# Where a feed-forward layer's first step takes its fourth weight operand from, and the order of the last tile's work before it

## The chip, the cores and the metric

The kernel runs on one core of one Trainium2 chip. Its metric is the time of one execution on the device in microseconds (us), lower is better. TensorE (PE in the profile) multiplies matrices, VectorE (DVE), ScalarE (ACT) and GpSimd (POOL) work on whole tiles of 128 partitions, and SP only issues transfers.

## The reference

One encoder layer over 1280 tokens (256 of a prompt, 1024 of a sample), width 1024. The change lies at the seam between the two steps below: the end of the attention part's output projection and the start of the FFN.

```python
    mix = jnp.concatenate([rmsnorm(a, mla_out_g), rmsnorm(b, na_out_g)], axis=-1)
    x = x + mix @ w_o
    h2 = rmsnorm(x, ffn_norm_g)
    x = x + (jax.nn.silu(h2 @ w_gate) * (h2 @ w_up)) @ w_down
```

All of it is float32: w_o is 1024 x 1024, w_gate and w_up are 1024 x 2816, w_down is 2816 x 1024.

## The kernel before

**Three matmuls for one.** Each float32 operand is split into a high half, a cast to the matmul type, and a low half, the raw value less the high half. `mm3` (L108) multiplies high by high (L110), high by low (L111) and low by high (L112). `split_S` (L890) does this for the token side, high by ScalarE (L892), low by VectorE (L893). `split_A` (L896) does it for weights, high by ScalarE (L899), low by GpSimd (L900), into six buffers named "wc".

**Seven products for eight.** Gate and up projections are done block by block with a seven-product scheme of fast matrix multiplication. Tokens fall into two halves of 640, the model width into two halves, and the columns go in pairs of 128: one step `fp` does a pair for gate (i = 0) and for up (i = 1), and there are eleven steps. For product m, TensorE multiplies a token operand S*m* by a weight operand. Operands of products 1 and 2 are blocks as they are ("11" and "12"), so they are free of sums; those of 6, 3, 5 and 7 are sums of blocks, which GpSimd builds (`sum_A`, L909, at L910). `product` (L966) does one half (s) of 320 tokens in 12 matmuls, so one operand has 24. The order is `SEQ = (1, 2, 6, 7, 4, 5, 3)`. Product 2 adds onto product 1's sum in PSUM (`CHAIN`), once ScalarE has copied that sum out (L980).

**The tiles before.** The loop at L936 walks over ten token tiles: `mix_T` and `out_proj` for the projection, then `ffn_in` (L840): x is squared (L844) and stored, `rstd_of` (L87) makes the reciprocal root on GpSimd (L89, L91), VectorE scales x (L847), TensorE transposes it (L856), VectorE and ScalarE scale the two transposed halves with the gains gf into the blocks R["11"] to R["22"] (L859, L863), named zA and zB in the trace. From tile 5 on, `difference` (L877) makes the block differences that the token operands need. T2[0] to T2[4], under the names A21, A22, sum, sum and A12, are the five cuts of S6, of 128 tokens each. Tile 8's are made by GpSimd, the last tile's by VectorE.

**The first FFN step.** Step 0 is written out by hand. Its first four operands are (gate, 1), (gate, 2), (up, 1) and (up, 2). Three are split while the tiles run (L941 to L945), which takes all six wc buffers; the block of the fourth, up's "12", is loaded at tile 7 into the buffer A12. The fourth is split inside the step:

```python
                if (i, m) == (1, 1):
                    w0[2, 1] = operand(A0[1], 2)
                    A0[1]["12"] = load_A(1, 0, "12", at[5])
                    w6 = [operand(A0[0], 6, at[6], "A21")]
                    hold = w6[0][2]
```

`hold` is the cast of gate's operand 6; the copies (L980) of the third and fourth operand's products come after it on ScalarE. The other blocks of step 0 and some of the sums lie in `at`, eight pieces of the two buffers that later hold S5. `build_S` (L1013) makes S6 (called at L1053), S7, S4, S5 and S3.

**Who sets the order.** SP's queue follows the program. On the other engines a planner lists the instructions before the run, by readiness as it reckons it and by program order; each engine then works through its list in order. `tc.issue_after(x)` puts what follows behind x in the planner's order. Pools are laid out end to end: the FFN pools (`l4a`: S6, 20 KB per partition; `l4z`: z, 20 KB; `l4b`: S5, S7, S4, 20 KB each) lie over the released pools of the tiles (gm and eight output weights of 8 KB, mT0 of 8 KB, then gf, three 4 KB buffers m and small ones, mT1, two x), and a buffer waits for those that it covers.

Of the kernel before, what the change touches and what calls it, by code (L numbers as in the profile page):

```python
# [11 lines left out]
F32 = mybir.dt.float32  # L12
F32R = mybir.dt.float32r
AF = mybir.ActivationFunctionType
# [25 lines left out]
def encoder_trunk(ctx: ExitStack, tc: tile.TileContext, x_tm, x_T, g_attn, w_c, w_v, w_qk,  # L40
# [46 lines left out]
    def rstd_of(out, ss, n):  # L87
        w = out.shape[1]
        nc.gpsimd.tensor_scalar(out=out, in0=ss, scalar1=1.0 / n, scalar2=EPS,  # L89
                                op0=ALU.mult, op1=ALU.add)  # L90
        nc.gpsimd.tensor_tensor(out=out, in0=out, in1=mhalf[:, 0:w], op=ALU.pow)  # L91

# [697 lines left out]

    mixed = [None]

# [47 lines left out]
    def ffn_in(t, x):  # L840
        h2 = rm.tile([P, D], F32, name="m", bufs=3)
        ss = rm.tile([P, 1], F32, name="ssh", bufs=2)
        r = rm.tile([P, 1], F32, name="rh", bufs=2)
        nc.scalar.activation(h2, x, AF.Square, accum_out=ss)  # L844
        store(xm_d[t], x)
        rstd_of(r, ss, D)
        nc.vector.tensor_scalar(out=h2, in0=x, scalar1=r, scalar2=1.0, op0=ALU.mult,  # L847
# [24 lines left out]
        difference(eng, R["11"][:, :, cs], R["12"][:, :, cs], R["11"][:, :, cs])  # L872
        difference(eng, T2[t - 5], R["22"][:, :, cs], R["11"][:, :, cs])
        if t < NT - 2:
# [21 lines left out]
    def split_A(raw):  # L896
        hi = rY.tile([P, 4, P], F32R, name="wc", bufs=6)
        lo = rY.tile([P, 4, P], F32R, name="wc", bufs=6)
        i0 = nc.scalar.copy(out=hi, in_=raw)  # L899
        i1 = nc.gpsimd.tensor_tensor(out=lo, in0=raw, in1=hi, op=ALU.subtract)  # L900
        return hi, lo, i0.ins, i1.ins
# [62 lines left out]

    l4 = [pool("l4a"), pool("l4z"), pool("l4b")]
    def product(C, w, m, s, held, bank=None, hold=None):  # L966
# [46 lines left out]
    def build_S(m, after):  # L1013
        pl, nm = {6: (l4[0], "S6"), 3: (rA, "zA")}.get(m, (l4[2], f"S{m}"))
        S[m] = [pl.tile([P, 4, NQ], F32R, name=nm, bufs=2) for x in "hl"]
        cuts = [(slice(n * P, (n + 1) * P), T2[n]) for n in range(5)] if m == 6 else [
            (slice(s * NS, (s + 1) * NS), None) for s in range(2)]
        for cs, from_ in cuts[:-1] if m == 6 else cuts:
            after = split_after(m, cs, from_, after)
        return after  # L1020
# [31 lines left out]

    s6 = build_S(6, ())  # L1053
    with tc.issue_after(s6[1]):
        cs8 = slice(3 * P, 4 * P)
        difference(nc.vector, R["21"][:, :, cs8], R["21"][:, :, cs8], T2[3])
    for fp in range(NF // 2):
# [3 lines left out]
        if fp == 0:  # L1061
            spare = [l4[2].tile([P, 4, NQ], F32R, name="S5", bufs=2).bitcast(F32)
                     .rearrange("p a b -> p (a b)").rearrange("p (n a b) -> p n a b", n=5, b=P)
                     for _ in range(2)]
            at = [spare[n // 5][:, n % 5] for n in range(8)]
            for n, (b, i) in enumerate((("21", 0), ("22", 0), ("21", 1), ("22", 1), ("12", 0),
# [3 lines left out]
            for i, m in ((0, 1), (0, 2), (1, 1), (1, 2)):  # L1070
                if (i, m) == (1, 1):
                    w0[2, 1] = operand(A0[1], 2)
                    A0[1]["12"] = load_A(1, 0, "12", at[5])
                    w6 = [operand(A0[0], 6, at[6], "A21")]
                    hold = w6[0][2]
                    s6 = split_after(6, slice(4 * P, 5 * P), T2[4], (hold, s6[1]))
                    with tc.issue_after(s6[1]):
                        difference(nc.vector, R["12"][:, :, cs8], R["22"][:, :, cs8],
                                   R["12"][:, :, cs8])
                        differences(nc.vector, NT - 1)  # L1080
# [307 lines left out]
```

## Time and profile before

| | us |
|---|---|
| median of 3 runs | 1619.09 |
| lowest and highest | 1615.41, 1620.34 |
| the profiled execution | 1617.07 |
| its span, first to last instruction | 1615.2 |

| engine | busy us | share of the span |
|---|---|---|
| PE matmul | 1582.2 | 98% |
| PE weight load | 1444.1 | 89% |
| DVE | 891.1 | 55% |
| ACT | 715.5 | 44% |
| POOL | 664.7 | 41% |

Shares are means over stages with different limits. The tile loop ends and the first FFN step begins at about 797 us of the span; the names M, z and zB (in L980, L982) mark the FFN's sums, S all token operands. The profile doesn't tell buffers of one name apart.

### The profile page before, as it was taken

The page shows a single profiled execution, that of the slowest core. Times are in us where ns is not written, and L with a number is a line of the kernel's source. Part 1 is how long each engine was busy: PE and PEld are TensorE (multiplying, and loading weights), DVE is VectorE, ACT ScalarE, POOL GpSimd, SP SyncE. Part 2 cuts the span into 40 slices and gives each one's busy share as a digit, 9 for nine tenths or more (in the row PEclk, how much of TensorE's full clock was granted, in tenths as well). Part 3 has the DMA queues.
Part 4 walks back from the last instruction along what each step waited for, and adds up shares of the span by engine and source line. Part 5 has one row for each costly group of instructions (what it writes and reads, how often), then busy time and mean ns, then how long its engine had stood idle before and what let it go on. Part 6 is the DMA issues. An engine that isn't in the chain of part 4 may idle for free.

```text
span 1615.2 us, 25739 instructions
## 1 busy us (share of the span) xinstructions
PE 1582.2 (98%) x9616; PEld 1444.1 (89%) x9616; DVE 891.1 (55%) x1483; ACT 715.5 (44%) x1484; POOL 664.7 (41%) x815
## 2 busy tenths in 40 slices
PE   8989999999999999999999999999999999999998
PEld 8978899998888888888899999999999998888886
DVE  5853054456677787533484444334444246886676
ACT  6533154455677777644353223232222332443334
POOL 4631434544211119224676665665656651010002
PEclk9999999999999999999999999999999999999999
DMA  8635202143101030233312232232332237843534
GB/s 293 200 90 141 49 24 63 35 168 102 32 16 30 21 113 16 92 118 143 118 58 72 97 110 93 62 100 84 101 110 70 76 128 264 298 140 97 157 103 155
DMA packets 123246, 171.12 MB, mean 106 GB/s; under 512 B 35504, under 2 KB 67504, under 8 KB 123120
## 3 DMA queue, kind: packets, MB, share of 16 engines
q1 hardware_dynamic: 78880, 120.30, 24.1%
q10 hardware_dynamic: 43680, 46.87, 8.4%
q0 software_dynamic: 560, 2.29, 0.3%
q8 instruction: 76, 1.25, 0.3%
q14 instruction: 50, 0.41, 0.1%
HBM read 118.96 MB, written 50.46 MB: 105 GB/s over the span
## 4 chain that ended last, share of the span: by engine, by line
PE 88%; DVE 3%; issue 2%; ACT 2%; POOL 2%; DMA 1%; ACTq 0%; SPq 0%; POOLq 0%; DVEq 0%
PE M L110 11%; PE M L112 11%; PE M L111 11%; PE d L111 5%; PE d L110 5%; PE d L112 5%; PE o L718 4%; PE tp L708 3%; PE na_o L489 2%; PE po L110 2%; PE po L111 2%; PE po L112 2%; PE pj L110 2%; PE pj L111 2%; PE pj L112 2%
## 5 line engine op out<-in xcount | busy, mean ns | idle before, releaser
L110 PE MATMUL M<-S,wc 128*128 128x320 f32 x1056 | 322.1, 310 | 2.5 <-ACT S L892 1.2
L111 PE MATMUL M<-S,wc 128*128 128x320 f32 x1056 | 324.3, 309 | 0.0
L112 PE MATMUL M<-S,wc 128*128 128x320 f32 x1056 | 312.1, 309 | 0.0
L110 PEld LDWEIGHTS M<-S,wc 128*128 128x128 f32 x1056 | 197.9, 188 | 3.7 <-ACT wc L899 1.6
L111 PEld LDWEIGHTS M<-S,wc 128*128 128x128 f32 x1056 | 198.8, 188 | 0.0
L112 PEld LDWEIGHTS M<-S,wc 128*128 128x128 f32 x1056 | 195.3, 188 | 0.0
L900 POOL TENSOR_TENSOR wc<-A,wc 128x512 fp32r<-128x512 f32 x86 | 120.6, 1403 | 81.5 <-ACT wc L899 81.4
L982 DVE TENSOR_TENSOR z<-M,z 128x320 f32<-128x320 f32 x120 | 56.6, 487 | 128.3 <-PE M L112 112.8
L899 ACT CAST wc<-A 128x512 fp32r<-128x512 f32 x86 | 53.5, 622 | 162.2 <-PE M L111 146.3
L900 POOL TENSOR_TENSOR wc<-sum,wc 128x512 fp32r<-128x512 f32 x62 | 88.6, 1430 | 85.7 <-ACT wc L899 85.7
L111 PE MATMUL d<-S,S 128*128 128x512 f32 (+1 forms) x314 | 121.2, 386 | 0.0
L112 PE MATMUL d<-S,S 128*128 128x512 f32 (+1 forms) x314 | 120.7, 386 | 0.0
L110 PE MATMUL d<-S,S 128*128 128x512 f32 (+1 forms) x314 | 120.4, 387 | 0.0
L982 DVE TENSOR_TENSOR zB<-M,zB 128x320 f32<-128x320 f32 x100 | 47.5, 488 | 131.7 <-PE M L112 125.3
L100 DVE TENSOR_TENSOR PT<-tp,PT 128x512 fp32r<-128x512 f32 (+1 forms) x144 | 93.0, 657 | 39.0 <-ACT PT L99 37.8
L899 ACT CAST wc<-sum 128x512 fp32r<-128x512 f32 x62 | 38.4, 619 | 143.2 <-PE M L111 94.5
L99 ACT CAST PT<-tp 128x512 fp32r<-128x512 f32 (+1 forms) x144 | 79.3, 565 | 38.3 <-PE tp L708 34.6
L700 DVE TENSOR_REDUCE mm<-S 128x1 f32<-128x1024 f32 (+1 forms) x80 | 84.8, 1061 | 10.9 <-PE S L112 9.3
L1029 ACT CAST S<-as 128x640 fp32r<-128x640 f32 x58 | 42.2, 728 | 105.6 <-issue 60.2
L702 ACT ACTIVATE ex<-S,mm 128x1024 f32<-128x1024 f32 (+1 forms) x80 | 79.7, 996 | 8.0 <-DVE mm L700 7.4
L731 POOL TENSOR_TENSOR ob<-ob 128x128 f32<-128x128 f32 x40 | 18.5, 462 | 157.3 <-ACT ob L728 153.8
L718 PE MATMUL o<-PT,v 128*128 128x256 f32 x544 | 80.6, 287 | 1.0 <-ACT PT L99 1.0
(429 smaller groups left out, 4118.1 us busy)
## 6 DMA issues: line engine op xcount, KB each, us to landing
as<-act_d SPq DMA_DIRECT2D x73, 320.0 KB
w<-in_w_down_dram SPq DMA_DIRECT2D x44, 256.0 KB
act_d<-z ACTq DMA_DIRECT2D x35, 320.0 KB
act_d<-zB ACTq DMA_DIRECT2D x35, 320.0 KB
A<-in_w_gate_dram SPq DMA_DIRECT2D x42, 256.0 KB
A<-in_w_up_dram SPq DMA_DIRECT2D x42, 256.0 KB
x<-in_x_tm_dram SPq DMA_DIRECT2D x20, 512.0 KB
cT_d<-stg ACTq DMA_DIRECT2D x20, 320.0 KB
```

Of the source, the lines that this page charges most:

```text
L99: i = nc.scalar.copy(out=hi, in_=ps)
L100: nc.vector.tensor_sub(out=lo, in0=ps, in1=hi)
L110: nc.tensor.matmul(out, lhsT=sh, rhs=mh, start=first, stop=False, **kw)
L111: nc.tensor.matmul(out, lhsT=sh, rhs=ml, start=False, stop=False, **kw)
L112: return nc.tensor.matmul(out, lhsT=sl, rhs=mh, start=False, stop=last, **kw).ins
L700: nc.vector.reduce_max(out=nm[:, u:u + 1], in_=S, axis=AX.X, negate=True)
L702: nc.scalar.activation(ex, S, AF.Exp, bias=nm[:, u:u + 1], scale=1.0, accum_out=l[:, u:u + 1])
L708: nc.tensor.transpose(tp[:, j], ex[:, kt * P:(kt + 1) * P], ident)
L718: nc.tensor.matmul(oT, lhsT=vv, rhs=pt[s][g][:, j], start=kt == 0 and s == 0, stop=kt == nkt - 1 and s == 1)
L899: i0 = nc.scalar.copy(out=hi, in_=raw)
L900: i1 = nc.gpsimd.tensor_tensor(out=lo, in0=raw, in1=hi, op=ALU.subtract)
L982: nc.vector.tensor_add(out=o, in0=ps, in1=a)
```

## The change

There are four edits. The second difference of tile 8, T2[3], is no longer made inside `ffn_in` but after the loop, on GpSimd still, behind the last tile's reciprocal root (`last_rs`). The first cast of S6 is put behind the last tile's square (`last_sq`). The fourth operand's halves get a place of their own, two pieces of the second S5 buffer, and are split before the step begins, the low half by VectorE. The pool of S5, S7 and S4 becomes three pools (`l4b`: two S5; `l4c`: S7's high half; `l4d`: two S4 and S7's low half), and the three pieces of `at` that lay in the second S5 buffer now lie in the first S4 buffer and in S7's high one.

```diff
--- before.py
+++ after.py
@@ -88,7 +88,7 @@
         w = out.shape[1]
         nc.gpsimd.tensor_scalar(out=out, in0=ss, scalar1=1.0 / n, scalar2=EPS,
                                 op0=ALU.mult, op1=ALU.add)
-        nc.gpsimd.tensor_tensor(out=out, in0=out, in1=mhalf[:, 0:w], op=ALU.pow)
+        return nc.gpsimd.tensor_tensor(out=out, in0=out, in1=mhalf[:, 0:w], op=ALU.pow).ins
 
     def split_w(hi, lo, raw):
         nc.gpsimd.tensor_scalar(out=hi, in0=raw, scalar1=1.0, scalar2=1.0, op0=ALU.mult,
@@ -788,7 +788,7 @@
             split_w(wt[:, 0], wt[:, 1], raw)
             wo.append(wt)
 
-    mixed = [None]
+    mixed, last_sq, last_rs = [None], [None], [None]
 
     def mix_in(t):
         ts_ = slice(t * P, (t + 1) * P)
@@ -841,9 +841,9 @@
         h2 = rm.tile([P, D], F32, name="m", bufs=3)
         ss = rm.tile([P, 1], F32, name="ssh", bufs=2)
         r = rm.tile([P, 1], F32, name="rh", bufs=2)
-        nc.scalar.activation(h2, x, AF.Square, accum_out=ss)
+        last_sq[0] = nc.scalar.activation(h2, x, AF.Square, accum_out=ss).ins
         store(xm_d[t], x)
-        rstd_of(r, ss, D)
+        last_rs[0] = rstd_of(r, ss, D)
         nc.vector.tensor_scalar(out=h2, in0=x, scalar1=r, scalar2=1.0, op0=ALU.mult,
                                 op1=ALU.mult)
         c0 = (t % 5) * P
@@ -870,7 +870,8 @@
         T2[t - 5] = rY.tile([P, 4, P], F32, name=nm, bufs=2 if nm == "sum" else 1)
         eng = nc.vector if t == NT - 1 else nc.gpsimd
         difference(eng, R["11"][:, :, cs], R["12"][:, :, cs], R["11"][:, :, cs])
-        difference(eng, T2[t - 5], R["22"][:, :, cs], R["11"][:, :, cs])
+        if t != NT - 2:
+            difference(eng, T2[t - 5], R["22"][:, :, cs], R["11"][:, :, cs])
         if t < NT - 2:
             differences(eng, t)
 
@@ -894,8 +895,7 @@
         return i0.ins, i1.ins
 
     def split_A(raw):
-        hi = rY.tile([P, 4, P], F32R, name="wc", bufs=6)
-        lo = rY.tile([P, 4, P], F32R, name="wc", bufs=6)
+        hi, lo = [rY.tile([P, 4, P], F32R, name="wc", bufs=6) for _ in range(2)]
         i0 = nc.scalar.copy(out=hi, in_=raw)
         i1 = nc.gpsimd.tensor_tensor(out=lo, in0=raw, in1=hi, op=ALU.subtract)
         return hi, lo, i0.ins, i1.ins
@@ -962,7 +962,7 @@
              4: ((1, 0), (0, 1)), 5: ((1, 1), (1, 1)), 3: ((0, 1), (0, 1))}
     DONE = {2: (0, 0), 4: (1, 0), 5: (1, 1), 3: (0, 1)}
 
-    l4 = [pool("l4a"), pool("l4z"), pool("l4b")]
+    l4 = [pool("l4a"), pool("l4z"), pool("l4b"), pool("l4c"), pool("l4d")]
     def product(C, w, m, s, held, bank=None, hold=None):
         bank = 1 - s if bank is None else bank
         if m not in CHAIN:
@@ -1011,8 +1011,9 @@
             (store_p if fp == NF // 2 - 1 else store)(act_d[n][fp], out)
 
     def build_S(m, after):
-        pl, nm = {6: (l4[0], "S6"), 3: (rA, "zA")}.get(m, (l4[2], f"S{m}"))
-        S[m] = [pl.tile([P, 4, NQ], F32R, name=nm, bufs=2) for x in "hl"]
+        pl, nm = {6: (l4[0], "S6"), 3: (rA, "zA"), 5: (l4[2], "S5")}.get(m, (l4[4], "S4"))
+        S[m] = [pl.tile([P, 4, NQ], F32R, name=nm, bufs=2) if m != 7 else
+                l4[3 + n].tile([P, 4, NQ], F32R, name="S7") for n in range(2)]
         cuts = [(slice(n * P, (n + 1) * P), T2[n]) for n in range(5)] if m == 6 else [
             (slice(s * NS, (s + 1) * NS), None) for s in range(2)]
         for cs, from_ in cuts[:-1] if m == 6 else cuts:
@@ -1050,26 +1051,35 @@
             split_f(w_ring[f], raw)
             ops[5, f] = a_ring[f], w_ring[f]
 
-    s6 = build_S(6, ())
+    def blocks(pl, nm, dt, bufs=2):
+        x = pl.tile([P, 4, NQ], F32R, name=nm, bufs=bufs)
+        x = (x.bitcast(F32) if dt is F32 else x).rearrange("p a b -> p (a b)")
+        x = x.rearrange("p (n a b) -> p n a b", n=5, b=P)
+        return [x[:, n] for n in range(5)]
+
+    at = blocks(l4[2], "S5", F32)
+    w0[2, 1] = hi, lo = blocks(l4[2], "S5", F32R)[0:2]
+    nc.scalar.copy(out=hi, in_=A0[1]["12"])
+    nc.vector.tensor_sub(out=lo, in0=A0[1]["12"], in1=hi)
+    b, c = blocks(l4[4], "S4", F32), blocks(l4[3], "S7", F32, 1)
+    at += [b[0], c[0], b[1]]
+    cs8 = slice(3 * P, 4 * P)
+    with tc.issue_after(last_rs[0]):
+        difference(nc.gpsimd, T2[3], R["22"][:, :, cs8], R["11"][:, :, cs8])
+    s6 = build_S(6, (last_sq[0],))
     with tc.issue_after(s6[1]):
-        cs8 = slice(3 * P, 4 * P)
         difference(nc.vector, R["21"][:, :, cs8], R["21"][:, :, cs8], T2[3])
     for fp in range(NF // 2):
         zp, zn = (rB, "zB") if fp % 2 else (l4[1], "z")
         G, U = C = [zp.tile([P, 2, NTOK], F32, name=zn, bufs=2) for _ in range(2)]
         held = ({}, {})
         if fp == 0:
-            spare = [l4[2].tile([P, 4, NQ], F32R, name="S5", bufs=2).bitcast(F32)
-                     .rearrange("p a b -> p (a b)").rearrange("p (n a b) -> p n a b", n=5, b=P)
-                     for _ in range(2)]
-            at = [spare[n // 5][:, n % 5] for n in range(8)]
             for n, (b, i) in enumerate((("21", 0), ("22", 0), ("21", 1), ("22", 1), ("12", 0),
                                         ("12", 1))):
                 A0[i][b] = load_A(i, 0, b, at[n]) if b != "12" or i == 0 else A0[i][b]
             hold = None
             for i, m in ((0, 1), (0, 2), (1, 1), (1, 2)):
                 if (i, m) == (1, 1):
-                    w0[2, 1] = operand(A0[1], 2)
                     A0[1]["12"] = load_A(1, 0, "12", at[5])
                     w6 = [operand(A0[0], 6, at[6], "A21")]
                     hold = w6[0][2]
```

## Rows read from the trace of the kernel before

**Rows 1.** The page, its part 1: each engine's busy time and share of the span

```profile
PE 1582.2 (98%) x9616; PEld 1444.1 (89%) x9616; DVE 891.1 (55%) x1483; ACT 715.5 (44%) x1484; POOL 664.7 (41%) x815
```

**Rows 2.** TensorE's waits: us in total, times, longest

```profile
PE M L110 <- ACT S L892: 1.2, 1, 1.2
PE M L110 <- ACT wc L899: 1.1, 2, 0.9
```

**Rows 3.** Busy time by stretch: stretch, its length, each engine's, clock, DMA

```profile
797.17:808.76 11.59, 11.59 (x81) 11.32 (x79) 10.38 (x9) 6.71 (x19) 10.92 (x9) 1.00 0.51 181
808.76:815.60 6.84, 4.73 (x20) 4.32 (x19) 5.96 (x5) 2.47 (x7) 6.76 (x5) 0.75 0.12 38
815.60:823.50 7.90, 7.90 (x56) 7.90 (x55) 6.70 (x5) 6.69 (x9) 7.90 (x5) 1.00 0.14 35
```

**Rows 4.** TensorE in order of time: start, us, line, what, wait before

```profile
809.65 0.41 PE L110 MATMUL M<-S,wc 128*128 128x320 f32 x1 [0.89 <-ACT wc L899]
...
811.44 0.83 PE L110 MATMUL M<-S,wc 128*128 128x320 f32 x2 [1.23 <-ACT S L892]
812.06 0.47 PE L111 MATMUL M<-S,wc 128*128 128x320 f32 x1
812.33 0.47 PE L112 MATMUL M<-S,wc 128*128 128x320 f32 x1
```

**Rows 5.** The chain that ended last, around the seam: start, us, work

```profile
798.05 1.54 ACT S L892 x3
799.59 1.06 ACT m L844 x2
...
802.05 1.88 DVE m L847
...
805.63 1.71 DVE zB L878
807.35 0.61 DVE zA L859
...
809.26 1.49 DVE A L878
810.77 0.63 ACT S L892
```

**Rows 6.** GpSimd in order of time, around the seam

```profile
798.62 1.82 POOL L878 TENSOR_TENSOR sum<-zB,zA 128x512 f32<-128x512 f32 x1
...
802.08 1.30 POOL L900 TENSOR_TENSOR wc<-A,wc 128x512 fp32r<-128x512 f32 x1
803.34 1.75 POOL L910 TENSOR_TENSOR sum<-S 128x512 f32<-128x512 f32 x1
...
808.47 1.72 POOL L910 TENSOR_TENSOR A<-S,S 128x512 f32<-128x512 f32 x1
...
816.93 1.76 POOL L910 TENSOR_TENSOR A<-S 128x512 f32<-128x512 f32 x1
```

**Rows 7.** ScalarE in order of time, around the seam

```profile
801.35 0.65 ACT L899 CAST wc<-A 128x512 fp32r<-128x512 f32 x1
...
816.08 2.42 ACT L892 CAST S<-zA 128x1280 fp32r<-128x1280 f32 x2
...
820.65 2.42 ACT L892 CAST S<-zB 128x1280 fp32r<-128x1280 f32 x2
```

**Rows 8.** VectorE in order of time, around the seam

```profile
798.59 2.40 DVE L893 TENSOR_TENSOR S<-A,S 128x512 fp32r<-128x512 f32 x2 [0.53 <-ACT S L892]
800.91 0.68 DVE L893 TENSOR_TENSOR S<-sum,S 128x512 fp32r<-128x512 f32 x1
...
803.85 1.79 DVE L893 TENSOR_TENSOR S<-sum,S 128x512 fp32r<-128x512 f32 x1
...
819.14 4.67 DVE L893 TENSOR_TENSOR S<-zA,S 128x1280 fp32r<-128x1280 f32 x2
```

**Rows 9.** SP's queue in order of time, around the seam

```profile
795.80 0.99 SPq L64 DMA_DIRECT2D S<-in_w_gate_dram  x2
```

## The prediction

> **What bounds the kernel now.** First the page: TensorE is busy for 98% of the span [rows 1], so only time in which it waits, or in which its clock is low, can be won. The table of its waits comes next. Around the edit, where the ten token tiles' output projection passes into the first FFN step, it has two waits worth naming, 0.89 us for a cast of an operand and 1.23 us for a cast of S [rows 2]. The third view, the busy times by stretch, prices this place. From 797.17 to 808.76 TensorE has no gap. From 808.76 to 815.60 it is busy for 4.73 of 6.84 us at a mean clock of 0.75. Afterwards it is full again, at full clock [rows 3]. At full clock one 320-column matmul follows the other every 0.147 us (7.90 us for 54 starts; the 56 of the row include two that run over its ends). In the poor stretch 18 start, worth 2.64 us, so 6.84 - 2.64 = **4.2 us are lost there**. They are made up of 0.89 + 1.23 of waits; of the half clock (0.75 as a mean of 1.0 and 0.5 means half of 6.84, 3.4 us, in which a matmul follows each 0.27 and some 12.7 of them cost 12.7 x 0.12 = 1.5); and of slow first matmuls after each wait, some 0.5 [rows 4].
>
> Which work ends last there is read from the chain of waits [rows 5]. It is the last tile: ScalarE casts three cuts of S6 (1.54) before the tile's square; square and rstd follow, then the scaling by VectorE; after that VectorE does two operations for the tile before (1.79 and 1.71, [rows 5, 8]), and only then the last tile's transposed half, its differences, and the cast of S6's fifth cut, on which TensorE waits until 811.44. One thing must be seen beside it. The fourth operand was not late: its low half is done at 802.08 + 1.30 = 803.38 [rows 6], five us before TensorE had nothing left. Its products wait because they add onto the sums of the third operand, whose copies out of PSUM are held behind the cast of operand 6, and because TensorE's list has three matmuls of operand 6 ahead of them.
>
> **The change, part by part.**
>
> *Square first.* The 1.54 us of casts leave the last tile's chain. If the fourth operand's high half is cast in their place, about 0.5 comes back (1.54 / 3). I take 1.4: rstd, and with it the scaling, at 800.65 in place of 802.05.
>
> *Tile 8's difference behind rstd.* The 1.82 us on GpSimd [rows 6] end before rstd could begin with the square late (the square ends at 799.59 + 1.06); with the square early they would have stood in front of it. Moved, this costs nothing on the chain; the two VectorE operations that use it must come later as well, so up to 3.5 us in front of the last tile's transposed half go too. The fifth cut can then be cast 1.4 to 4.9 us earlier. Either figure covers the 1.23 wait.
>
> *Fourth operand.* Its place is over weights that the last output matmul reads, so its high half can be cast from 797.2 on, not 801.35 [rows 7]. The low half leaves GpSimd (1.30) and costs VectorE between 0.68, what such a subtraction took with GpSimd nearly idle, and 1.79, what another took beside full GpSimd work [rows 8]. Six cast buffers now serve three operands, so operand 6 takes a pair that is free at about 800.7 (24 matmuls of 0.147 after 797.17) and can be cast when its sum is there. That sum and the one before it follow tile 8's difference on GpSimd: 800.65 + 1.82 + 2 x 1.75 = 806.0, the cast is done 0.6 later, and TensorE has other work until 808.76. The 0.89 wait goes.
>
> *Buffers.* A sum of gate now lies where S7's high half is built, one of up where S4 is built. Casts of S7 begin at 816.08 and of S4 at 820.65 [rows 7]; the last readers of the sums, on GpSimd, are done at 808.47 + 1.72 and 816.93 + 1.76 [rows 6]. So 5.9 and 2.0 us cover this. Without the cover S4 would be late, which is wanted only two operands (48 matmuls, 7.0 us) after S7. The reload of up's block 12 goes to S4's buffer, which lies over the gains that the last tile's scaling reads until 807.35 + 0.61. SP's queue has nothing but the next step's loads behind it. Its reader is the sum at 816.93, 9 us later; a load asked for at 795.80 was read at 803.34 [rows 6, 9], so 7.5 us is an upper bound. Zero.
>
> *What is late next.* Without the loss TensorE comes to S7's products at 819.3 (18 + 54 matmuls after 808.76 they start at 823.5; less 4.2). S7's low halves are VectorE's, two of 2.37 us, done at 819.14 + 4.67 = 823.8 [rows 8]. VectorE has 3.3 us idle in all from 797.17 to 823.5 (11.59 - 10.38, 6.84 - 5.96, 7.90 - 6.70 [rows 3]). Some 2.3 of it, behind the scaling, can be closed, as work no longer waits for TensorE. But the casts of S6 now stand behind the square, so the three subtractions, which began at 798.59, begin at 800 or so: 1.4 us that VectorE does not get back, with the fourth operand's low half (0.7) inside this gap at best. S7 is then done at 823.8 - 2.3 + 1.4 = 822.9. The ends: 822.1 (2.5 closed, 0.8 lost) and 826.1 (0.9 closed, 1.4 lost and 1.79 added).
>
> How much later than 823.8 TensorE wanted S7's second half is not in the trace. It is between 0 (there is no wait) and 3.5 us (24 matmuls of the first halves of gate and up ahead). I take 1.3, nearer to 0, since its list mixed products at 808 to 812. The gain is then 823.8 + 1.3 - 822.9 = **2.2 us**: of 4.2 won in the seam, 2.0 become a wait for VectorE's S7. Later steps of the kernel aren't touched, and TensorE is full there, so it stays to the end. The profiled execution took 1617.07 (its span 1615.2 and 1.9 around it); 2.2 less is 1614.9. The median of the three runs is 2.02 higher, at 1619.09, so I forecast **1616.9**.
>
> **The rivals.**
>
> *All of it* (22 in 100). If VectorE comes at its early end (S7's halves at 819.7 and 822.1) and TensorE's list takes the first halves of gate and up together (3.5 us from 819.3), at most 0.4 of waiting is left. Without it 4.2 are won: 1614.9. For it: VectorE's idle 3.3 us are there to be closed. Against: the subtractions' later start.
>
> *Nothing to speak of* (18). Either TensorE's list still puts operand 6 ahead of the fourth operand, or the new wait of 2.0 brings the half clock again, as the 2.1 us of waits were followed by it here: 2.2 - 1.5 = 0.7, so 1618.4.
>
> *Slower* (15). VectorE and GpSimd hold each other up. A subtraction that took 0.68 beside small GpSimd work took 1.79 beside large, and GpSimd's 1.30 became 1.72 to 1.82 [rows 6, 8]. If what counts is the sum of both, an idle VectorE is no reserve, since GpSimd has 0.7 us idle in the 26 [rows 3]. The change then empties 798.6 to 800.6: the difference (1.30) and two subtractions (1.36) go into the full stretch, the fourth operand is worth 1.30 - 0.68 = 0.6 less, and S7 is done 2.1 later, at 825.9. It decides from 825.1 on, TensorE's present need: 0.8 slower, 1619.9. The Trainium skill's page "SBUF — State Buffer", section "Who interferes with whom", states this as an exclusive lock: a VectorE operation with two SBUF inputs and a GpSimd operation that reads SBUF don't overlap at all. By it a pair would take 0.68 + 1.30 = 1.98, an estimate; the rows show pairs of about 1.75, so they overlap a little, which keeps the chance low. The time by that rule would be this rival's.
>
> **How the numbers follow.** The forecast has 45 in 100, its own span 1615.7 to 1618.2. About 0.3%, 4.9 us, is what a measurement here can tell from no change; the three runs lie 4.9 apart. Faster by more needs all of the 4.2 and 0.7 of luck: four tenths of 22 and one tenth of 45, so 0.13. Slower by more: 0.05, from the slow rival's bound (S7 at 826.1) and luck. Within: 0.82. The range reaches from the full gain with 1.3 us of run spread, 1613.6, to the slow rival with 0.7, 1620.6.
>
> **What would show it.** The profile after should have no wait of TensorE at its fourth operand and no low clock at 812; the last tile's square at about 798.1, before the S6 casts; its transposes some 2 us earlier; a subtraction of the fourth operand on VectorE at 0.7 to 1.8 us; and a wait on "S" from VectorE before S7's first products near 819 to 823. The forecast is wrong if that wait is absent (4.2 won), if the half clock shows again, or if S7's last low half ends later than 825.1.

## The result: slower, by a wait that the prediction did not name

The changed kernel takes 1624.97 us (median of 12 runs, 1622.13 to 1628.37) against 1619.38 of the kernel before on the same chip (12 runs); the ratio is 1.0033, 95% interval 1.0024 to 1.0042. A second measurement on another occasion gave 1.0027 [1.0015, 1.0038]. The forecast was 1616.9, a gain of 2.2 us.

In the profiled execution, 1624.95 us with a span of 1623.2, the page still has TensorE busy for 98%:

```profile
PE 1585.1 (98%) x9616; PEld 1446.6 (89%) x9616; DVE 886.9 (55%) x1484; ACT 716.7 (44%) x1484; POOL 661.6 (41%) x814
```

That says as little as [rows 1] did. The table of TensorE's waits says more. The wait for a cast of S in [rows 2] is gone, that for "wc" is down from 0.9 to 0.7, and a new one for GpSimd's "wc" has come, 3.9 us at one stroke:

```profile
PE M L112 <- POOL wc L900: 4.3, 2, 3.9
PE M L110 <- ACT wc L899: 0.7, 1, 0.7
```

All times below are counted from the step's start, which is 797.17 in the profile before and 801.20 here (the 4.0 us between come from earlier stages and are dealt with under the run of the kernel before). The busy times by stretch, to be held against [rows 3] (columns as there):

```profile
801.20:820.00 18.80, 18.63 (x129) 18.36 (x127) 16.39 (x15) 9.99 (x26) 15.50 (x12) 1.00 0.42 127
820.00:829.30 9.30, 4.90 (x19) 4.64 (x20) 6.63 (x7) 6.11 (x7) 8.93 (x5) 0.66 0.11 30
829.30:837.20 7.90, 7.90 (x55) 7.90 (x54) 5.13 (x7) 3.48 (x4) 3.73 (x2) 0.97 0.00 0
```

The hole of 6.84 us that lay 11.6 us after the start has closed: TensorE is full, at full clock, for 18.8 us. Then comes a hole of 9.3 us, in which 19 matmuls start instead of 63, and the clock's mean is 0.66. TensorE in order of time shows what it is made of ([rows 4] before):

```profile
820.48 0.42 PE L110 MATMUL M<-S,wc 128*128 128x320 f32 x1 [0.65 <-ACT wc L899]
...
825.25 0.63 PE L112 MATMUL M<-S,wc 128*128 128x320 f32 x1 [3.92 <-POOL wc L900]
825.68 0.47 PE L110 MATMUL M<-S,wc 128*128 128x320 f32 x1
...
829.15 0.47 PE L110 MATMUL M<-S,wc 128*128 128x320 f32 x1
829.42 0.45 PE L111 MATMUL M<-S,wc 128*128 128x320 f32 x1
829.68 0.33 PE L112 MATMUL M<-S,wc 128*128 128x320 f32 x1
829.85 0.30 PE L110 MATMUL M<-S,wc 128*128 128x320 f32 x1
...
863.12 0.41 PE L112 MATMUL M<-S,wc 128*128 128x320 f32 x1 [0.41 <-POOL wc L900]
```

A wait of 3.92 for the low half of up's operand 6, and behind it some 4 us in which a matmul follows each 0.267 us, the half clock, and not each 0.147. Matched by their number in the step, the matmuls run 4.4 us ahead of those of the kernel before at 15 to 18 us after the start, so the seam's 4.2 were won. From 29 us on they run 2.7 behind: the hole took 7.1. Another 0.7 go 62 us after the start, at the last line's wait for another low half. The chain of waits, where [rows 5] had the last tile's scaling, now runs through GpSimd into that wait:

```profile
818.13 1.71 POOL S L910 x2
...
821.43 1.28 POOL A L910
822.72 2.49 POOL wc L900
825.25 0.63 PE M L112
```

GpSimd's own list, against [rows 6]:

```profile
804.53 1.49 POOL L879 TENSOR_TENSOR sum<-zB,zA 128x512 f32<-128x512 f32 x1
807.85 1.67 POOL L910 TENSOR_TENSOR sum<-S 128x512 f32<-128x512 f32 x1 [1.83 <-DVE S L894]
809.60 1.65 POOL L910 TENSOR_TENSOR S<-sum,A 128x512 f32<-128x512 f32 x1
811.20 1.75 POOL L910 TENSOR_TENSOR S<-A,S 128x512 f32<-128x512 f32 x1
812.91 1.75 POOL L910 TENSOR_TENSOR A<-S,S 128x512 f32<-128x512 f32 x1
814.62 1.73 POOL L900 TENSOR_TENSOR wc<-S,wc 128x512 fp32r<-128x512 f32 x1
816.31 1.74 POOL L910 TENSOR_TENSOR sum<-S 128x512 f32<-128x512 f32 x1
818.13 1.65 POOL L910 TENSOR_TENSOR S<-sum,A 128x512 f32<-128x512 f32 x1
819.73 1.76 POOL L910 TENSOR_TENSOR S<-A,S 128x512 f32<-128x512 f32 x1
821.43 1.28 POOL L910 TENSOR_TENSOR A<-S 128x512 f32<-128x512 f32 x1
822.65 6.28 POOL L900 TENSOR_TENSOR wc<-S,wc 128x512 fp32r<-128x512 f32 x3
```

Read it as a list of nine operations that has to be worked off before TensorE gets what it wants: for gate the two sums of operand 6, operand 7's sum, operand 3's, the low half of operand 6; for up the same four sums, and then the low half, the first of the last row's three. The first sum starts 6.65 us after the step's start (807.85 - 801.20); before, with the fourth operand's low half still in front, it started after 6.17 (803.34 in [rows 6]). So the work that left GpSimd bought nothing: the sum then stood idle for 1.83 behind VectorE.

ScalarE and VectorE against [rows 7] and [rows 8]:

```profile
801.95 0.64 ACT L1062 CAST S<-A 128x512 fp32r<-128x512 f32 x1
...
802.46 1.09 ACT L844 ACTIVATE m<-x 128x1024 f32<-128x1024 f32 x1
...
803.51 1.15 ACT L893 CAST S<-A 128x512 fp32r<-128x512 f32 x2
804.54 0.64 ACT L893 CAST S<-sum 128x512 fp32r<-128x512 f32 x1
...
813.54 0.62 ACT L893 CAST S<-A 128x512 fp32r<-128x512 f32 x1 [0.66 <-DVE A L879]
```

```profile
802.62 0.69 DVE L1063 TENSOR_TENSOR S<-A,S 128x512 fp32r<-128x512 f32 x1 [0.53 <-ACT S L1062]
804.17 0.69 DVE L894 TENSOR_TENSOR S<-A,S 128x512 fp32r<-128x512 f32 x1 [0.86 <-ACT S L893]
804.78 1.79 DVE L847 TENSOR_SCALAR m<-x,rh 128x1024 f32<-128x1024 f32 x1
806.49 0.68 DVE L894 TENSOR_TENSOR S<-A,S 128x512 fp32r<-128x512 f32 x1
807.10 1.28 DVE L894 TENSOR_TENSOR S<-sum,S 128x512 fp32r<-128x512 f32 x2
...
821.62 2.44 DVE L894 TENSOR_TENSOR S<-zA,S 128x1280 fp32r<-128x1280 f32 x1 [0.90 <-ACT S L893]
...
824.39 2.16 DVE L894 TENSOR_TENSOR S<-zA,S 128x1280 fp32r<-128x1280 f32 x1
```

The square stands where it was meant to, ahead of the casts of S6. But the third cut's subtraction, the first of the two "S<-sum,S" at 807.10, now follows the scaling of the last tile and another cut, and the first sum writes into the "sum" buffer that this subtraction reads. It ends at about 807.74; the sum starts at 807.85. Last, SP's queue ([rows 9]): the gate and up blocks of step 0 are asked for from 801.39 on, 0.2 after the step's start, not 1.4 ahead of it.

```profile
801.39 1.71 SPq L64 DMA_DIRECT2D S<-in_w_gate_dram  x2
```

The two S5 buffers have changed places, and the blocks now lie over the output weights that the last output matmul reads. So there were two suspects for the late first sum, the buffer and the loads.

### The profile page after: what moved, and what is told of

Same layout as the page of the kernel before. It is cut to its first block, busy times and chain, and to the rows that moved or that the text cites. A ratio compares the mean times of both kernels' runs of the same rounds, so it can differ in the third digit from the quotient of the medians.

```text
span 1623.2 us, 25742 instructions
## 1 busy us (share of the span) xinstructions
PE 1585.1 (98%) x9616; PEld 1446.6 (89%) x9616; DVE 886.9 (55%) x1484; ACT 716.7 (44%) x1484; POOL 661.6 (41%) x814
## 3 DMA queue, kind: packets, MB, share of 16 engines
q1 hardware_dynamic: 78880, 120.30, 24.1%
## 4 chain that ended last, share of the span: by engine, by line
PE 85%; DMA 5%; POOL 3%; ACT 2%; DVE 2%; issue 2%; SPq 1%; ACTq 0%; POOLq 0%; DVEq 0%
PE M L112 10%; PE M L110 10%; PE M L111 10%; PE d L110 5%; PE d L111 5%; PE d L112 5%; PE o L718 4%; PE tp L708 3%; PE po L110 2%; PE po L111 2%; PE po L112 2%; PE na_o L489 2%; PE pj L110 2%; PE pj L111 2%; PE pj L112 2%; PE S L110 2%
```

## The experiments

A measure for each: how many matmuls run in the 69 us from the step's start. At full clock each is worth 0.147 us, and the count leaves out what other stages do. Before it is 444, after it 421: 23 x 0.147 = 3.4 us lost in this one step.

| kernel | us | before, same chip | ratio, 95% interval | matmuls | TensorE's waits there, us |
|---|---|---|---|---|---|
| before, again | 1619.16 | 1618.62 | 1.0000 [0.9989, 1.0011] | 445 | 2.1 |
| after, again | 1623.28 | 1618.62 | 1.0027 [1.0015, 1.0038] | 420 | 5.0 |
| places only | 1619.88 | 1620.53 | 1.0000 [0.9991, 1.0010] | 433 | 2.8 |
| without the square | 1622.54 | 1619.77 | 1.0012 [1.0001, 1.0023] | 424 | 3.5 |
| without tile 8's move | 1622.91 | 1619.77 | 1.0019 [1.0008, 1.0029] | 425 | 4.9 |
| two sums left out | 1617.41 | 1618.62 | 0.9984 [0.9972, 0.9996] | 465 | 1.1 |
| S5 places exchanged | 1621.56 | 1619.93 | 1.0014 [1.0002, 1.0026] | 425 | 4.5 |
| third cut first | 1621.76 | 1620.53 | 1.0012 [1.0002, 1.0022] | 429 | 4.0 |
| low halves first | 1620.72 | 1620.53 | 0.9999 [0.9990, 1.0008] | 440 | 2.9 |
| the last two together | 1619.81 | 1620.53 | 1.0007 [0.9996, 1.0017] | 429 | 2.8 |
| exchanged, third cut first | 1622.13 | 1619.77 | 1.0021 [1.0008, 1.0033] | 431 | 4.0 |
| and operand 3's sums last | 1621.86 | 1619.77 | 1.0013 [1.0003, 1.0022] | 419 | 4.7 |
| sums in order of need | 1620.21 | 1618.62 | 1.0005 [0.9993, 1.0016] | 435 | 2.4 |
| and a difference behind S7 | 1621.43 | 1619.93 | 1.0008 [0.9996, 1.0019] | 433 | 2.9 |
| and a low half sooner | 1618.73 | 1619.54 | 0.9996 [0.9987, 1.0006] | 448 | 1.8 |

Nearly every kernel here is the changed one with an edit. The counts come from one profile each. What a ratio says and what its count says lie up to 1.9 us apart, with either sign, and the intervals of neighbouring ratios overlap; where two of these kernels are compared with each other, the argument rests on the counts and the waits.

**Both kernels once more.** No edit.

> The kernel before, unchanged, profiled and timed once more. Theory (the 2 to 4 us by which every later profile lags that of before ahead of the step are differences from run to run, not the change): its profile too lags by 1 us or more at 400 us, with the same program; the ratio's interval holds 1.000. Rival (the change's places shift the stages ahead of the step): it lags by under 0.5 us. At the step the two waits of 0.9 and 1.2 us are there again, and none at operand 6's low halves.

> The changed kernel once more. Theory: ratio 1.002 to 1.004, and in its profile the wait of about 4 us at the low half of up's operand 6 again; the step loses 2.5 to 3.5 us against before's. Rival (the first measurement was a high one): ratio under 1.0015.

Before has its two waits again, 0.89 and 1.22, and 445 matmuls; after has its 3.9 again (3.91), and 420. The step repeats to a matmul. The stages ahead of it don't: before's second profile begins the step at 799.77, 2.6 us later than the first. Instruction by instruction it runs 0.2 late at 350 us and 2.6 late from 370 on, so the lag that was expected at 400 us is there with the same program. Most of the 4.0 us in front of after's step can be such differences; no cause for them was sought.

**Which edit.** Three kernels take parts of the change back. Places only:

```diff
-        if t != NT - 2:
-            difference(eng, T2[t - 5], R["22"][:, :, cs], R["11"][:, :, cs])
+        difference(eng, T2[t - 5], R["22"][:, :, cs], R["11"][:, :, cs])
...
-    with tc.issue_after(last_rs[0]):
-        difference(nc.gpsimd, T2[3], R["22"][:, :, cs8], R["11"][:, :, cs8])
-    s6 = build_S(6, (last_sq[0],))
+    s6 = build_S(6, ())
```

> The changed kernel without two of its edits: tile 8's difference is made inside the loop again, and S6's casts aren't held behind the last tile's square; the fourth operand's place and the pools stay. GpSimd theory: three cuts of S6 are split before the last tile's scaling, so the buffer is free in time and the first sum starts 1.8 us earlier than in the changed kernel (0.5 us earlier against the start of the step than in the kernel before); the wait at up's operand 6 falls to about 2.8 us, ratio 1.0012 to 1.0022. A second theory, that the place itself costs (VectorE has one operation more and the pools let transfers in late): the wait stays over 4 us and the ratio at 1.003.

The second kernel takes only the last line back (square behind the casts), the third only the others (tile 8's difference at its own tile).

> The changed kernel with its places, its VectorE split and its move of tile 8's difference, but with the last tile's square back behind the casts. Theory (GpSimd's list of sums is the bound, and the square first puts the third cut's split, whose buffer the first sum needs, behind it): the first sum no longer waits for that split, but rstd's two operations and the difference behind them come later in the same list, so the list is moved little: time within 0.2% of the changed kernel's 1625, TensorE still short of 3 to 4 us at the low halves of up's operand 6. Rival (the square's place alone makes the loss, by VectorE's and ScalarE's order): 1620, as the kernel without the square and without the move measured. Rival (noise of the first 400 us only): no difference from the kernel before.

> The changed kernel with tile 8's difference back at its own tile, the square still first. Theory: GpSimd's list at the step begins without that difference (1.5 us), but its first sum still waits for the load that lands 5.9 us after the step's start and for the third cut's split: first sum at most 0.5 us sooner, time 1624 to 1625. Rival (the move is what costs, since 1.5 us were pushed behind rstd into a full list): 1.5 to 2 us faster, 1623.

Places only give no difference (1.0000, under the theory's 1.0012 to 1.0022; by the count 1.6 us are lost): TensorE waits 2.3 us for the same low half and 0.5 for a cast, about what the old waits cost. Its first sum starts 6.22 after that run's start (807.73 - 801.51), 0.4 sooner than in after and not 1.8, for it waits 1.75 for a VectorE difference. On top of the places each of the other two edits makes it worse by the counts: 433 matmuls with neither, 424 with the move, 425 with the square, 420 or 421 with both. With the move and without the square the first sum no longer waits, but stands behind a rstd that is late: 805.64, 6.15 after that run's start at 799.49. There the expectation missed the place of TensorE's waits: 2.0 us of them are at a cast that stands behind S7's casts, 0.7 at S7, and only 0.6 at low halves of operands. With the square and without the move it waits 2.07 for the same split and starts after 6.59: beside the square the move changes little, since it falls into the hole in GpSimd's list.

**Is it GpSimd's list?** The two sums of operand 3 are left out of step 0:

```diff
-            sum_A(A["s4"], A["12"], A["s2"])
+            if s4:
+                A["s4"] = A["s1"]
+            else:
+                sum_A(A["s4"], A["12"], A["s2"])
```

> The changed kernel without the two sums that make operand 3 of step 0 (3.5 us of GpSimd's list ahead of the low half of up's operand 6 and behind it); operand 3 is cast from another sum instead, so its values are not the reference's. Theory (GpSimd's list is what TensorE waits for): the low half of up's operand 6 comes 3 us sooner, the wait of 3.9 us is under 1 us, those of operand 7 gone, time 1620.5 to 1622. Rival (VectorE's own list, S7's halves, holds TensorE right behind): a wait of 1.5 us or more moves to S7, time 1623 to 1625.

1617.41, and 465 matmuls, 21 more than before, or 3.1 us gained in the step. One wait is left:

```profile
PE M L112 <- POOL wc L900: 1.1, 1, 1.1
```

```profile
800.08:820.00 19.92, 19.23 (x133) 18.95 (x131) 17.50 (x16) 12.39 (x28) 16.62 (x12) 1.00 0.37 120
820.00:829.30 9.30, 8.88 (x60) 8.89 (x61) 9.30 (x8) 6.40 (x9) 9.13 (x5) 1.00 0.34 115
829.30:837.20 7.90, 7.90 (x56) 7.90 (x55) 7.34 (x11) 4.54 (x6) 3.80 (x3) 1.00 0.11 41
```

3.5 us less work on GpSimd brings 44 matmuls, 6.5 us: the wait, and the half clock behind it, which is not there (clock 1.00 throughout). The time is lower than the theory's 1620.5 to 1622, which had put the gain at about the work left out. So GpSimd's list stood in the way of the change. What the kernel before would gain without these two sums was not run, so the 3.1 us can't be put down to the change's idea alone. VectorE's S7, the forecast's next wait, costs nothing here; with less work on GpSimd it is also done sooner, 24.1 us after the start and not 25.4.

**What holds the list's first sum?** The loads, by an exchange of the two S5 places:

```diff
-    at = blocks(l4[2], "S5", F32)
-    w0[2, 1] = hi, lo = blocks(l4[2], "S5", F32R)[0:2]
+    at = blocks(l4[2], "S5", F32, 1)
+    w0[2, 1] = hi, lo = blocks(l4[3], "S5", F32R, 1)[0:2]
```

(with each S5 buffer in a pool of its own), and the buffer, by splitting the third cut first:

```diff
+        if m == 6:
+            cuts = [cuts[2], cuts[0], cuts[1], cuts[3], cuts[4]]
```

> The changed kernel with nothing but the two places exchanged: the gate and up blocks of step 0 in the lower place, as before, the fourth operand's halves in the upper. Theory (the first sum waits for two things, the blocks' landing and the buffer that the third cut's split frees, 0.1 to 0.7 us apart): loads 1.6 us sooner, but the first sum only 0.1 to 0.7 us sooner, the wait at the low half of up's operand 6 still 3.2 to 3.9 us, time 1623 to 1625. Rival (the landing alone is the cause): first sum 1.5 us or more sooner, wait under 2.5 us, time 1621 to 1622.

> S6's third cut (T2[2], whose buffer GpSimd's first sum of gate's operand 6 needs) is split first of the four. GpSimd theory (TensorE's new wait of 0.65 + 3.92 us at up's operand 6 is GpSimd's list: it stood 1.83 us for that buffer, then had nine operations ahead of that low half): the first sum starts right behind tile 8's difference, 1.8 us earlier against the start of the step, the two waits shrink from 4.6 to about 2.8 us, and the time falls by 1.8 to 3 us from the changed kernel's 1625 (ratio to the kernel before 1.0014 to 1.0022). VectorE theory (S7's low halves, or the turns of VectorE and GpSimd, set the end): what the first sum gains comes back as a wait for S before S7's products, and the time stays within 0.7 us of 1625.

> The changed kernel with two edits: the gate and up blocks of step 0 in the lower of the two places (as before) and the hi and lo halves of the fourth operand in the upper, and the third cut of operand 6 split first. Theory (the first sum waited for the blocks' landing, which the place over the last output weights delays, and then for the third cut's buffer): loads issued 1.5 us before the step's start instead of 0.2 after, first sum 4 to 5 us after the step's start instead of 6.7, the wait at the low halves of up's operand 6 down from 3.9 to 2 us or less, time 1618 to 1620.5; the third cut first alone gave 1621.8. Rival (VectorE's casts and GpSimd's count of operations bind, not where the list begins): as the third cut first alone, 1621 to 1622, the wait only moved to the low halves of S7.

With the exchange the blocks are asked for at 798.62, 1.4 us before that step's start at 800.00, and nothing else moves:

```profile
798.62 0.80 SPq L64 DMA_DIRECT2D S<-in_w_gate_dram  x2
```

```profile
806.65 1.67 POOL L910 TENSOR_TENSOR sum<-S 128x512 f32<-128x512 f32 x1 [1.83 <-DVE S L894]
```

First sum 6.65 after the start, and TensorE's wait is 3.91 as ever. So the loads, though late, did not hold the list; the buffer did. (The time, 1621.56, fell into the rival's range all the same; that run has 4 matmuls more than after because the wait of 0.4 some 62 us after the start is missing.) With the third cut first the sum starts 5.66 after (804.36 - 798.70), and now it does wait for the loads, 0.84; with both edits 4.78 (807.94 - 803.16). The wait at up's low half is then gone, but the step gains only 8 to 10 matmuls: 2.3 and 1.7 us, or 2.7 and 1.2, are waited for high halves behind late S7 casts and for S7's low halves. So the expectation of both edits held for the first sum and for the wait at the low half; that for the time didn't, and the rival had it.

**The list in another order.** First, operand 6's low halves ahead of the sums that operands 7 and 3 need, without and with the third cut first:

```diff
-            sum_A(A["s4"], A["12"], A["s2"])
+            with ExitStack() as es:
+                if s4:
+                    es.enter_context(tc.issue_after(w[3]))
+                sum_A(A["s4"], A["12"], A["s2"])
...
-                w = w6 if m == 6 else [operand(A0[i], m) for i in range(2)]
+                with ExitStack() as es:
+                    if m == 7:
+                        es.enter_context(tc.issue_after(w6[1][3]))
+                    w = w6 if m == 6 else [operand(A0[i], m) for i in range(2)]
```

> GpSimd's sums for operand 7 and the fourth sums of gate and up stand behind the low half of operand 6 in its list, so up's low half is its seventh operation of the step and not its tenth. GpSimd theory: that low half is done some 5 us earlier (three operations of 1.75), the wait of 3.92 us at up's operand 6 is gone; the low half of gate's operand 7 keeps its place in the list, so a wait of 2 to 3 us for it (GpSimd wc) comes instead, and the time falls by 1.5 to 3.5 us (ratio 1.001 to 1.0023). VectorE theory: the wait moves to S before S7's products, some 3 us of it, and the time falls by at most 1 us.

> The two edits together: third cut first, and the low halves of operand 6 ahead of the other sums. GpSimd theory: both gains add, the waits in the seam come to 1 us or less, the half clock does not show, and the time is 5 to 7 us under the changed kernel's (ratio to the kernel before 0.9988 to 1.0003), so that it is level with the kernel before or beats it. VectorE theory: S7's low halves are done at the same time as in the changed kernel, TensorE waits 2 to 3 us for S, and the ratio stays over 1.0015.

The wait for the low half falls to 0.5 us and none, and 2.4 and 2.8 come at the casts of operand 7, whose sums now stand at the list's end. Even so the first of the two kernels has 440 matmuls, 19 or 20 more than after, and a ratio of 0.9999: this order alone won most of the loss back. With the third cut first besides, the count is 429, so the two gains did not add. Then, on the exchange and the third cut first, operand 3's two sums last, their second operand in S4's buffer:

> The edits of the run before and GpSimd's sums in the order of their need: for gate and up first the two sums and the low half of operand 6, then the two sums of operand 7 and its low halves, and the sums that make operand 3 last (their buffer in S4's place, so that S7's cast doesn't wait for them). Theory (list's order and start are the bound): low halves of up's operand 6 done some 17 us after the step's start, those of operand 7 by 25; all long waits of TensorE in the step below 1 us, no stretch of half clock, time 1616 to 1618, 2 to 4 us below the kernel before. Rival (VectorE's low halves of S7, done 24 us after the step's start at the earliest, bind next): a wait of 1 to 2 us there, time 1618 to 1620.

It missed both ways. The second sum, which now writes that buffer, stood 3.3 us behind ScalarE's work for the last tile (L863), and S4's low halves waited 1.3 for the sums put last. Up to 43 us after the start it has lost no more than before; then VectorE and GpSimd are late, and a wait of 2.2 us 61 us after the start has half clock behind it. Next, the changed kernel's buffers with the order gate's two sums, low half, operand 3's sum; up's two sums, low half; operand 7's two sums; up's sum for operand 3; operand 7's low halves:

> The changed kernel with the blocks of step 0 in the lower place, the third cut first, and GpSimd's sums in the order of their need with the buffers as the change has them: for gate two sums, the low half of operand 6 and operand 3's sum, for up two sums and the low half, then operand 7's sums, up's sum for operand 3, operand 7's low halves. Theory (list's start and order): first sum 4.8 us after the step's start, low half of up's operand 6 at 16, of operand 7 at 23 and 24.5, no wait over 1 us in the step, and no low half of S4 held back; time 1617 to 1619. Rival (VectorE and GpSimd share what bounds them, so each order only moves the wait to VectorE's differences, S7 and S4): waits of 2 us or more in sum between 20 and 60 us after the step's start, time 1619 to 1621.5.

First sum and up's low half came when the theory said, 4.8 and 16.4 us after the start, operand 7's 0.9 later (23.9); then VectorE's S7 was waited for, 0.5 and 1.9 us. The rival had it. The next kernel moves a VectorE difference, which only S4 needs, behind S7's low halves:

```diff
-                        differences(nc.vector, NT - 1)
+                        z9 = difference(nc.vector, R["12"][:, :, cs9], R["22"][:, :, cs9],
+                                        R["12"][:, :, cs9])
...
+                        with tc.issue_after(low[1]):
+                            difference(nc.vector, R["21"][:, :, cs9], R["21"][:, :, cs9], T2[4])
```

> The run with lower place, third cut first and sums in the order of their need, and besides it one of VectorE's differences of the last tile, which only S4 needs (1.8 us), behind the low halves of S7. Theory (GpSimd's list no longer binds there; the 1.9 us at S7's second low half are VectorE's list, one operation too long): waits at S7's low halves 2.4 us down to under 0.8, S4 not late, time 1618 to 1619, 1 to 2 us below the run without this edit. Rival (VectorE and GpSimd are full together, so the wait only moves on to S4's halves or operand 7's): 1.5 us or more of waits in sum from 820 to 845, time as without the edit, 1620.

No gain: 1.0 us is left at S7, and 1.8 come at operand 7's low half for gate, which stands behind operand 3's sum for up (2.5 us beside VectorE's work). The last kernel changes these two over:

```diff
-                    A = A0[1]
-                    with tc.issue_after(last):
-                        last = sum_A(A["s4"], A["12"], A["s2"]).ins
-                    with tc.issue_after(last):
-                        w = [operand(A, 7, 0) for A in A0]
+                    w = []
+                    for A in A0:
+                        with tc.issue_after(last):
+                            w.append(operand(A, 7, 0))
+                        last = w[0][3]
+                        if len(w) == 1:
+                            with tc.issue_after(last):
+                                last = sum_A(A0[1]["s4"], A0[1]["12"], A0[1]["s2"]).ins
```

> The run before this one with VectorE's difference behind S7, and besides it operand 7's low half for gate ahead of operand 3's sum for up in GpSimd's list. Theory (each engine's list, in the order in which TensorE needs it, is what sets the end): that low half is done 2.5 us sooner and the wait of 1.8 us for it goes; the wait of 1.0 us at S7's second low half stays; if the half-clock stretch behind the two goes as well, as it did in the kernel without two of the sums, the step gains 2 to 3.5 us and the time is 1616.5 to 1618.5, under both kernels. Rival (the sum that is moved back now delays S4's low halves or operand 7's second one by as much): a wait of 1.5 us or more there, time 1620 to 1621.5.

```profile
PE M L111 <- DVE S L894: 1.0, 1, 1.0
PE M L112 <- POOL wc L900: 0.7, 1, 0.7
```

448 matmuls, 0.6 us better than before in the step, and 1618.73: the loss of the change is undone, and no gain is left over (0.9996 [0.9987, 1.0006]). The 1.8 us of waits are again followed by half clock (mean 0.86 over the 12 us around them). The theory's 1616.5 to 1618.5 was just missed. No version that does all the work beats the kernel before by more than the measurement can tell.

## Why the prediction was wrong, point by point

*Square first, tile 8's difference:* right. The scaling began 3.58 us after the start (804.78), forecast 3.48. The fifth cut's cast came 12.3 after instead of 13.6 (810.77 in [rows 5]): 1.3 sooner, just short of the 1.4 to 4.9. The wait of 1.23 went.

*Fourth operand:* right in what it removes; its low half took VectorE 0.69, the lower bound. Wrong in the sentence "That sum and the one before it follow tile 8's difference on GpSimd: 800.65 + 1.82 + 2 x 1.75 = 806.0", which is 8.83 after the start. They ended at 811.25, 10.05 after. The step overlooked that the first of them takes over the buffer of the third cut. The prediction did say that the three subtractions would now begin later, and charged it to VectorE alone.

*Buffers:* right, zero; the later loads, which it had not seen, cost nothing as the run with the places exchanged shows.

*What is late next:* this is the step that failed. It followed VectorE to S7, and rightly so far: forecast 822.9, which is 25.7 after the start, measured 824.39 + 2.16 = 826.55, 25.4 after. But TensorE has another operand to take before S7, up's operand 6, and GpSimd's list up to its low half was not followed past gate's. In the kernel before, that low half and the first matmul that reads it, the 125th of the step (the one that waits in after), are

```profile
818.65 1.29 POOL L900 TENSOR_TENSOR wc<-S,wc 128x512 fp32r<-128x512 f32 x1
```

```profile
820.59 0.31 PE L112 MATMUL M<-S,wc 128*128 128x320 f32 x1
```

The low half was done at 819.94, 22.8 after the start, and TensorE came for it 23.4 after: 0.6 us to spare, while the change was to bring TensorE there 4.2 us sooner, at 19.2. From the end of gate's second sum (805.16 + 1.64 in that trace) to the start of the low half there are seven operations, 818.65 - 806.80 = 11.85 us. So even from the prediction's own 806.0 the low half would have begun at 817.85 and ended at 819.14, 22.0 after the start. A wait of 2.8 us followed from the trace of the kernel before.

It became 3.92. The low half was done 24.0 after (822.65 + 2.55 = 825.20), 2.0 later than that: gate's second sum ended 1.2 later (10.05 - 8.83), the seven operations took 11.4, 0.45 less, and the low half itself took 2.55 and not 1.29, 1.26 more, as it now ran beside VectorE's first subtraction for S7 (821.62, 2.44 long). TensorE for its part asked 20.1 after (825.25 - 3.92 - 801.20) and not 19.2, as it had first waited 0.65 for the high half of the same operand. The low half began 21.5 after the start in both kernels; what changed is that TensorE was there first. The waits of the kernel before hid this list; with 4.2 us of them gone, TensorE met it.

The S7 wait that was forecast is not in after, nor in the run with two sums left out. It is there, 1.0 to 2.4 us, in five of the kernels in which up's low half came in time (third cut first, with and without the exchange, and the last three), so VectorE was close behind, as the forecast said.

*Rivals.* "Slower" had the sign, by a neighbouring mechanism: VectorE and GpSimd are full together, but the operand that came late was GpSimd's operand 6 and not S7, and the price was 3.4 us of the step, not 0.8. Its mechanism had a share of 1.26 us, the low half that took 2.55 beside VectorE. The return of the half clock stood under "nothing to speak of"; here it came with a wait twice as long as the one that it was reckoned with.

What stays open: by its ratios the kernel is 4.4 to 5.3 us slower, by its counts 3.4 to 3.7 in the step. From the step's start to the last instruction the profiles of before take 818.0 and 817.6 us, those of after 822.0 and 822.1, 4.2 more in the mean. Matmul by matmul nothing more is lost between the step and 1290 us; behind that the profiles part by 0.4 to 0.5, but so do the two of before. The rest is no larger than in other runs of the table, where it has both signs, so scatter may be all of it.

## What to carry to other kernels

When a stall is to be removed, follow every engine's list up to the next operand that the waiting engine takes, and not only the engine that seems fullest: ask of each how much time it has to spare once the consumer comes sooner by the whole gain. When two instructions change places, look for what reuses the buffers of the one that moves back. Where two engines are both full, a new order mostly moves the wait: here the best orders got back to the kernel before (440 and 448 matmuls against 444), and only less work (two sums, 3.5 us) went clearly beyond it (465).

## What the runs showed of the hardware

VectorE's subtractions and GpSimd's sums slow each other to one pace. In the kernel with the sums in order of need two VectorE subtractions took 3.49 us beside GpSimd sums, and the next, begun while GpSimd stood idle for 0.73, took 0.68:

```profile
806.43 3.49 DVE L894 TENSOR_TENSOR S<-A,S 128x512 fp32r<-128x512 f32 x2
809.85 0.68 DVE L894 TENSOR_TENSOR S<-sum,S 128x512 fp32r<-128x512 f32 x1
```

```profile
805.92 1.74 POOL L910 TENSOR_TENSOR sum<-S 128x512 f32<-128x512 f32 x1
807.74 1.64 POOL L910 TENSOR_TENSOR S<-sum,A 128x512 f32<-128x512 f32 x1
810.10 1.58 POOL L900 TENSOR_TENSOR wc<-S,wc 128x512 fp32r<-128x512 f32 x1 [0.73 <-ACT wc L899]
```

A pair takes about 1.75, less than 0.68 + 1.30 = 1.98. The Trainium skill's page "SBUF — State Buffer", section "Who interferes with whom", has the two exclude each other, by which it would be the 1.98, an estimate; the trace shows a little overlap. Beside VectorE's 1280-element subtractions a 512-element operation of GpSimd took 2.52 to 2.55 (in after, and in the kernels with the sums in order of need).

The half clock adds to what the waits cost. In after the 15 matmuls from 825.68 to 829.68 cost 0.12 more each, 1.8 us, behind waits of 0.65 and 3.92; in the kernel with two sums left out a wait of 1.10 was followed by none.
